# Attention scores over all 128 rows: zero-filled query tiles for each head, and the decay as two rows of k

## The chip, the cores and the metric

The kernel runs on one core of one Trainium2 chip. The metric is the device time of one execution in microseconds (us). The engines are named in the profile as PE (TensorE matmuls), PEld (TensorE weight loads), DVE (VectorE), ACT (ScalarE), POOL (GpSimd) and SP (SyncE, which issues most transfers).

## The reference, cut to what matters

A decoder trunk of two layers over 512 tokens of width 1024. The even layer has two groups of heads side by side, the odd layer has one; each layer ends in an expert-retrieval part (PEER), which the change leaves alone. Heads are 64 wide.

```python
# even layer, group A: 8 heads; an indexer picks the keys that a query may use
li = einsum('bthd,bsd->bths', q_idx, k_idx) * 64 ** -0.5          # 8 indexer heads, one shared k
iscore = einsum('bths,bth->bts', relu(li), w_idx)                 # top 128 keys of it are kept
s = q_lat . ckv * 64 ** -0.5 + bias(dist)                         # scores of group A on the kept keys
# even layer, group B: 4 heads, two softmax maps each, difference of the two
# odd layer, forgetting attention: 16 heads
cum = cumsum(log_sigmoid(f_logit), axis=1)
s = einsum('bthd,bshd->bhts', q, k) * 64 ** -0.5 + cum[t] - cum[s]
p = softmax(where(s_pos <= t_pos, s, -1e30))
```

The term `cum[t]` is the same for all keys of a query and drops out of the softmax; the kernel adds only `-cum[s]`.

## The kernel before

Tokens lie in four blocks of 128. Projections give q and k transposed: a chunk of 128 output columns holds two heads of 64, in partitions 0 to 63 and 64 to 127, with the 512 tokens along the free axis. Where precision matters a tensor is kept as a pair, its fp32r rounding and the rest (`split`, `split_to`: one ScalarE copy, lines 161 and 164, and one VectorE subtraction, lines 162 and 165), and a product is three fp32r passes (`mm3`, lines 147 to 149). Group A and group B take plain fp32 copies of q and k, where a product shows as two instructions of TensorE (line 465).

A unit is one head and one block of queries. Its scores (`scores`, line 459) contract over the 64 partitions of the head, with q as the stationary operand of 64x128 and up to 512 keys moving. There are 24 indexer units (8 heads, blocks 1 to 3), 32 units of group A, 32 matrices of group B and 64 units in the odd layer. After the scores of a group A unit one more pass adds the mask of the kept keys (line 760). After those of an odd unit one more pass adds the decay: `selR` is a constant tile of ones and zeros that picks the two rows of head h out of `cum` (its rounding in row h, its rest in row 32 + h), so line 1013 is a fourth pass over all 128 partitions. `selR` is loaded as two transfers of 512 KB ahead of the odd attention (lines 983 to 986).

Units run as a software pipeline of four or five steps (`run_units`): scores with mask and exp, the division by the sum, the transpose, the product with v. Between units a filler issues steps of the projections still to come (1.8 a unit in the odd layer), and a background list issues steps of the adaLN sums of the next sub-layers: 64 loads of 128x512 in the odd layer, two a unit, each with one VectorE instruction (lines 237 to 241). q and k of a pair of heads have two buffers each, so the projections run up to one pair ahead. The adaLN loads have three buffers of their own in the odd layer (`araw`), the projection weights have three raw buffers (`raw`, in `stream`) and three for each half of the split. The order of instructions on every engine and queue is fixed when the kernel is built, by a scheduler that follows the order of the program and its own costs; `issue_after` puts an instruction behind another one.

Lines that the prediction names: 161, 162 (splits), 465 (fp32 scores), 495 (transposes), 729 (a 128-row fp32 product with ones, in group A's stage), 800 (the copy of 64x512 out of PSUM), 1013 (the decay pass).

## Time and profile before

| What | Value |
|---|---|
| Median of three runs | 3238.81 us (3231.16 to 3241.28) |
| Profiled execution | 3246.8 us, span 3245.0 us |
| PE busy | 3159.7 us, 97% of the span |
| PEld busy | 2698.1 us, 83% |
| DVE busy | 2564.9 us, 79% |
| ACT busy | 1355.3 us, 42% |
| POOL busy | 683.2 us, 21% |
| Mean granted TensorE clock | 0.987 of full speed |

The rows come from one profiled execution, and the times in them are counted from the start of its span. A matmul's row gives its start and a modelled end; matmuls overlap in the pipeline, so the pace of TensorE is read from start to start. By the starts of the score instructions the indexer lies at 57 to 110 us, group B at 143 to 215, group A at 232 to 322 and the odd attention at 1709 to 1928.

### The profile page before, as it was taken

To read this page: it belongs to the slowest core of one execution; us is meant where nothing else is said; L and a number is where in the kernel's file an instruction comes from. 1 tells how busy PE (TensorE), PEld (TensorE's weight loads), DVE (VectorE), ACT (ScalarE), POOL (GpSimd) and SP (SyncE) were. 2 spreads that over 40 slices of the span, in tenths; PEclk is the share of its full clock that TensorE was granted. 3 is DMA by queue.
4 is the path that set the end of the run, shared out by engine and by line. 5 is a ranking of instruction groups with operands and counts; after the bars stand their busy time and mean duration, and the time that the engine had idled before them with its cause. 6 is when DMAs were issued, how large, how long until landed. Compare 5 with 4: busy or idle time off the path is not lost.

```text
span 3245.0 us, 45265 instructions
## 1 busy us (share of the span) xinstructions
PE 3159.7 (97%) x16480; PEld 2698.1 (83%) x16480; DVE 2564.9 (79%) x5076; ACT 1355.3 (42%) x2254; POOL 683.2 (21%) x516
## 2 busy tenths in 40 slices
PE   8999899999999999999999999999999999999998
PEld 4765788998999999887877778899988899899877
DVE  5887799997688877788757657999867777787877
ACT  4466423553333333333455564245533333333333
POOL 0000000002344444443200000000023444444331
PEclk9999999999999999999999989999999999999999
DMA  7314523568799899999645212246588999899885
GB/s 239 124 53 150 197 86 103 214 228 283 270 330 329 320 335 324 316 323 319 234 146 170 91 63 87 98 158 226 210 292 294 324 324 334 316 319 329 312 298 201
DMA packets 303967, 759.89 MB, mean 234 GB/s; under 512 B 24008, under 2 KB 124928, under 8 KB 297600
## 3 DMA queue, kind: packets, MB, share of 16 engines
q1 hardware_dynamic: 225536, 481.09, 43.1%
q0 software_dynamic: 73728, 268.47, 22.8%
q10 hardware_dynamic: 4480, 7.44, 0.7%
q8 instruction: 129, 2.11, 0.3%
q14 instruction: 94, 0.77, 0.1%
HBM read 700.01 MB, written 56.64 MB: 233 GB/s over the span
## 4 chain that ended last, share of the span: by engine, by line
PE 61%; DMA 17%; DVE 13%; issue 6%; ACT 2%; POOL 1%; SPq 0%; DVEq 0%; ACTq 0%; POOLq 0%
DMA gv<-in_peer_v_dram,eidx 9%; PE ups L149 7%; PE ups L147 7%; PE ups L148 7%; PE y L148 6%; PE y L149 6%; PE y L147 6%; PE pp L147 3%; PE pp L149 3%; PE pp L148 3%; DVE wl L162 3%; DMA raw<-in_peer_v_dram 2%; DMA gu<-in_peer_u_dram,eidx 1%; PE gps L1169 1%; DMA raw<-in_peer_uT_dram 1%
## 5 line engine op out<-in xcount | busy, mean ns | idle before, releaser
L161 ACT ACTIVATE wh<-raw 128x1024 fp32r<-128x1024 f32 x598 | 631.6, 1056 | 1026.0 <-PE ups L148 457.8
L162 DVE TENSOR_TENSOR wl<-raw,wh 128x1024 fp32r<-128x1024 f32 x598 | 728.8, 1219 | 140.4 <-ACT wh L161 138.6
L1406 POOL DMA_INDIRECT gu<-in_peer_u_dram,eidx x256 | 287.0, 1121 | 1964.4 <-DVE eidx L1265 1514.7
L149 PE MATMUL ups<-h2h,wl 128*128 128x384 f32 x2048 | 692.8, 338 | 6.4 <-DVE wl L162 6.4
L147 PE MATMUL ups<-h2h,wh 128*128 128x384 f32 x2048 | 693.6, 339 | 3.6 <-ACT gl L1046 2.4
L148 PE MATMUL ups<-h2l,wh 128*128 128x384 f32 x2048 | 689.7, 337 | 0.0
L147 PE MATMUL y<-wh,weh 128*128 128x512 f32 x1536 | 602.4, 392 | 12.9 <-ACT weh L161 7.2
L148 PE MATMUL y<-wl,weh 128*128 128x512 f32 x1536 | 605.5, 394 | 7.9 <-DVE wl L162 7.6
L149 PE MATMUL y<-wh,wel 128*128 128x512 f32 x1536 | 604.4, 394 | 0.0
L1406 POOL DMA_INDIRECT gv<-in_peer_v_dram,eidx x256 | 396.0, 1547 | 549.2 <-DVE gu L1413 358.5
L1421 DVE SCALAR_TENSOR_TENSOR acc<-gv,act,acc 128x1024 f32<-128x1024 f32 x256 | 328.0, 1281 | 164.6 <-DMA gv<-in_peer_v_dram,eidx 164.1
L147 PEld LDWEIGHTS ups<-h2h,wh 128*128 128x128 f32 x2048 | 385.8, 188 | 11.9 <-ACT gl L1046 3.1
L149 PEld LDWEIGHTS ups<-h2h,wl 128*128 128x128 f32 x2048 | 385.4, 188 | 9.9 <-DVE wl L162 9.8
L148 PEld LDWEIGHTS ups<-h2l,wh 128*128 128x128 f32 x2048 | 385.9, 188 | 6.5
L1413 DVE SCALAR_TENSOR_TENSOR gu<-gu,htm 128x1024 f32<-128x1024 f32 x256 | 311.9, 1219 | 51.9 <-DMA gu<-in_peer_u_dram,eidx 51.6
L147 PEld LDWEIGHTS y<-wh,weh 128*128 128x128 f32 x1536 | 290.6, 189 | 73.1 <-ACT weh L161 8.5
L148 PEld LDWEIGHTS y<-wl,weh 128*128 128x128 f32 x1536 | 290.2, 189 | 71.7 <-DVE wl L162 13.8
L161 ACT ACTIVATE weh<-wf 128x384 fp32r<-128x384 f32 x256 | 133.7, 524 | 498.3 <-PE y L148 345.2
L149 PEld LDWEIGHTS y<-wh,wel 128*128 128x128 f32 x1536 | 290.2, 189 | 61.9 <-DVE wel L162 1.3
L162 DVE TENSOR_TENSOR wel<-wf,weh 128x384 fp32r<-128x384 f32 x256 | 141.4, 553 | 83.1 <-ACT weh L161 82.6
L1300 DVE TENSOR_TENSOR wf<-gl,gt 128x384 f32<-128x384 f32 x256 | 139.9, 551 | 9.5 <-DMA gt<-gates 8.9
L1046 ACT ACTIVATE gl<-ups 128x384 f32<-128x384 f32 x256 | 121.4, 474 | 0.1
(388 smaller groups left out, 4251.5 us busy)
## 6 DMA issues: line engine op xcount, KB each, us to landing
raw<-in_peer_uT_dram SPq DMA_DIRECT2D x256, 512.0 KB
raw<-in_peer_v_dram SPq DMA_DIRECT2D x256, 512.0 KB
araw<-in_ada_w_dram SPq DMA_DIRECT2D x192, 256.0 KB
gates<-gst SPq DMA_DIRECT2D x48, 1024.0 KB
gt<-gates SPq DMA_DIRECT2D x32, 1536.0 KB
raw<-in_peer_wq_dram SPq DMA_DIRECT2D x32, 512.0 KB
raw<-in_odd_w_dram SPq DMA_DIRECT2D x25, 512.0 KB
raw<-in_even_w_dram SPq DMA_DIRECT2D x23, 512.0 KB
```

Of the source, the lines that this page charges most:

```text
L147: mm(out, a[0], b[0], start=start, stop=False)
L148: mm(out, a[0], b[1], start=False, stop=False)
L149: mm(out, a[1], b[0], start=False, stop=stop)
L161: self.lact = nc.scalar.activation(hi, src, AF.Copy)
L162: self.last = nc.vector.tensor_tensor(lo, src, hi.bitcast(F32), op=ALU.subtract)
L1046: nc.scalar.activation(gl, ps[:, :ND], AF.Gelu_apprx_tanh)
L1169: nc.tensor.matmul(ps[:, z], oh[:, t, 1], og[:, t, 0], start=True, stop=False)
L1300: nc.vector.tensor_tensor(wf.rearrange("p (c t) -> p c t", t=CT), gls[i].rearrange("p (c t) -> p c t", t=CT), self.gt[:, :, i % IG], op=AL ...
L1406: nc.gpsimd.indirect_dma_start(out=r, out_offset=None, in_=table, in_offset=bass.IndirectOffsetOnAxis(ap=eidx[:, k:k + 1], axis=0))
L1413: nc.vector.scalar_tensor_tensor(r, r, 1.0, htm, op0=ALU.mult, op1=ALU.mult, accum_out=act[:, k:k + 1])
L1421: nc.vector.scalar_tensor_tensor(acc, r, act[:, j:j + 1], acc, op0=ALU.mult, op1=ALU.add)
```

## The change

Each head gets its own query tile of 128 partitions, with the head's 64 rows in place and zeros in the other 64 (`head_tiles`). The zeros are written once by GpSimd; the split then writes only the head's half, so a split of 128 partitions becomes two of 64. Scores contract over all 128 partitions (`scores_full`), so the other head's rows of k meet zeros. This is done in the indexer (two generations of tiles), in group A (two) and in the odd layer (two); group B keeps its 64 rows.

In the odd layer k has a tile for each head too. In the half that the head doesn't use, the first two rows of the query tile are set to one, and the two rows of `cum` for the head are copied into the same rows of the k tile by a transfer from GpSimd's queue. The decay pass, `selR`, its two loads and its input go.

To make room, the adaLN loads of the odd layer take the shared `raw` buffers, `fT` takes one as well, and the latent's scratch `ckv` lies in `oT`, which is written only later.

```diff
+            qa = [self.head_tiles(qkp, f"qa{g}", 1, F32) for g in range(2)]
+            qz = []
+            def proj_i(b, w=None):
                 ps = self.bank(psum, "pp")
-                yield from self.proj_s_steps(chunk, hT, ps, w)
-                return self.split(qkp, [P, T], ps, tag, scale=scale)
+                yield from self.proj_s_steps(W[1 + b], hT, ps, w)
+                q = qz[b % 2]
+                for j in range(2):
+                    r = slice(j * HD, (j + 1) * HD)
+                    self.split_to(q[j][0][r], q[j][1][r], ps[r])
+                return q
+            def proj_aq(i):
...
+                    nc.scalar.activation(q[j][0][r], ps[r], AF.Copy, scale=HD ** -0.5)
...
+                    qz += [self.head_tiles(ix, f"qz{g}", 2) for g in range(2)]
...
-                        sc = self.scores(q, k, j * HD, tb, psum, last=tb == 0)
+                        sc = self.scores_full(q[j], k, tb, psum, last=tb == 0)
...
-        ckv = pool.tile([P, NTB, 256], F32, name="ckv")
+        ckv = self.oT[:, 0:2].rearrange("p a (b c) -> p (a b) c", c=256)
...
-                c["sc"] = self.scores(fl.get(f"i{h // 2}"), ki, (h % 2) * HD, tb, psum)
+                c["sc"] = self.scores_full(fl.get(f"i{h // 2}")[h % 2], ki, tb, psum)
...
+    def head_tiles(self, pool, name, parts, dt=F32R):
+        heads = []
+        for j in range(2):
+            tiles = [pool.tile([P, T], dt, name=self.nm(f"{name}{z}{j}"), bufs=1) for z in "hl"[:parts]]
+            for a in tiles:
+                self.nc.gpsimd.memset((a if dt == F32 else a.bitcast(F32))[(1 - j) * HD:(2 - j) * HD], 0.0)
+            heads.append(tiles)
+        return heads
+    def scores_full(self, q, k, tb, psum, last=True):
+        ps = self.bank(psum, "sc")
+        n = (tb + 1) * P
+        t = slice(tb * P, (tb + 1) * P)
+        if len(q) == 1:
+            self.nc.tensor.matmul(ps[:, :n], q[0][:, t], k[0][:, :n], start=True, stop=last)
+        else:
+            self.mm3(ps[:, :n], (q[0][:, t], q[1][:, t]), (k[0][:, :n], k[1][:, :n]), True, last)
+        return ps
...
-            selR = mp.tile([P, 16, P], F32R, name="selR")
-            qkp = s2.enter_context(self.pool("qk", bufs=2))
+            qkp = s2.enter_context(self.pool("qk"))
+            gens = [[self.head_tiles(qkp, x, 2) for x in "qk"] for g in range(2)]
+            for q, k in gens:
+                for j in range(2):
+                    nc.gpsimd.memset(q[j][0].bitcast(F32)[(1 - j) * HD:(1 - j) * HD + 2], 1.0)
...
-                fT = fp.tile([16, T], F32, name="fT")
+                fT = self.stream.tile([P, D], F32, tag="raw", name=self.nm("fT"))[:16, :T]
...
-                for z in range(2):
-                    raw = self.load(I["sel"][:, z * D:(z + 1) * D])
-                    with self.tc.issue_after(lead[0]), self.tc.issue_after(lead[1]):
-                        nc.scalar.activation(selR[:, z * 8:z * 8 + 8].rearrange("p a b -> p (a b)"), raw, AF.Copy)
...
+            def proj_qk(i):
+                q, k = gens[i % 2]
+                for x, chunk, scale in ((q, W[i], HD ** -0.5), (k, W[8 + i], None)):
+                    ps = self.bank(psum, "pp")
+                    yield from self.proj_s_steps(chunk, hT, ps)
+                    for j in range(2):
+                        r = slice(j * HD, (j + 1) * HD)
+                        self.split_to(x[j][0][r], x[j][1][r], ps[r], scale)
+                for j in range(2):
+                    h, o = 2 * i + j, (1 - j) * HD
+                    nc.gpsimd.dma_start(k[j][0].bitcast(F32)[o:o + 2], cum.bitcast(F32)[h:h + 33:32])
                 return q, k
...
-            self.bg = [self.ada(layer, m, ah, psum) for m in (2, 4, 3, 5)]
+            self.bg = [self.ada(layer, m, ah, psum, "tr", 0) for m in (2, 4, 3, 5)]
...
-                    sc = self.scores(q, k, j * HD, tb, psum, last=False)
-                    nc.tensor.matmul(sc[:, :n], selR[:, 2 * i + j], cum[:, :n], start=False, stop=True)
+                    sc = self.scores_full(q[j], k[j], tb, psum)
```

## Rows read from the trace of the kernel before

**Rows 1.** Busy time by stage; the first line names the columns.
```profile
core 0: us, PE busy (x) PEld busy (x) DVE busy (x) ACT busy (x) POOL busy (x), PEclk, DMA share, GB/s
...
57.00:110.00 53.00, 53.00 (x259) 37.91 (x258) 33.04 (x59) 23.04 (x47) 0.00 (x0) 1.00 0.38 125
110.00:143.00 33.00, 33.00 (x152) 26.61 (x150) 31.36 (x79) 11.24 (x15) 0.00 (x0) 1.00 0.45 145
143.00:215.00 72.00, 70.78 (x323) 47.22 (x324) 69.58 (x209) 46.63 (x117) 0.00 (x0) 1.00 0.15 52
...
232.00:322.00 90.00, 86.00 (x343) 50.61 (x342) 64.70 (x153) 58.77 (x149) 0.00 (x0) 0.96 0.42 139
...
1640.00:1675.00 35.00, 32.67 (x153) 26.41 (x151) 19.87 (x36) 21.42 (x39) 0.00 (x0) 1.00 0.41 135
...
1709.00:1800.00 91.00, 91.00 (x434) 67.92 (x434) 70.81 (x167) 49.82 (x121) 0.00 (x0) 0.96 0.53 176
1800.00:1860.00 60.00, 60.00 (x282) 43.52 (x280) 37.04 (x92) 34.13 (x82) 0.00 (x0) 0.95 0.22 71
1860.00:1928.00 68.00, 65.63 (x288) 47.80 (x288) 35.40 (x94) 40.70 (x99) 0.00 (x0) 0.87 0.10 32
```

**Rows 2.** Timeline of PE, an odd unit: start us, duration us, instruction.
```profile
1845.98 0.40 PE L149 MATMUL pp<-hTh,wl 128*128 128x512 f32 x1
1846.31 0.49 PE L147 MATMUL sc<-kh,qh 64*128 64x512 f32 x1
1846.64 0.39 PE L148 MATMUL sc<-kl,qh 64*128 64x512 f32 x1
1846.88 0.39 PE L149 MATMUL sc<-kh,ql 64*128 64x512 f32 x1
1847.19 0.50 PE L1013 MATMUL sc<-cum,selR 128*128 128x512 f32 x1
1847.53 0.38 PE L495 MATMUL tr<-ident,e 128*128 128x128 f32 x2
...
1848.91 0.39 PE L149 MATMUL pp<-hTh,wl 128*128 128x512 f32 x1
1849.14 0.40 PE L147 MATMUL pp<-hTh,wh 128*128 128x512 f32 x1
```

**Rows 3.** Timeline of PE, an indexer unit between projection passes.
```profile
93.46 0.28 PE L149 MATMUL pp<-wh,hTl 128*128 128x256 f32 x1
93.67 0.49 PE L147 MATMUL sc<-kih,qh 64*128 64x512 f32 x1
...
94.55 0.39 PE L147 MATMUL pp<-wh,hTh 128*128 128x256 f32 x1
94.78 0.28 PE L148 MATMUL pp<-wl,hTh 128*128 128x256 f32 x1
```

**Rows 4.** Timeline of PE, fp32 products in group A's stage.
```profile
248.49 1.12 PE L465 MATMUL sc<-kf,qf 64*128 64x512 f32 x2
249.55 1.12 PE L729 MATMUL tr<-rdg,ones 128*128 128x512 f32 x2
250.51 0.60 PE L495 MATMUL tr<-ident,e 128*128 128x128 f32 x4
```

**Rows 5.** Groups of instructions: busy us, mean ns of one, idle before.
```profile
L800 ACT ACTIVATE oT<-pp 64x512 f32<-64x512 f32 x24 | 14.2, 590 | 19.5 <-PE pp L149 10.4 <-PE pp L509 8.9
...
L162 DVE TENSOR_TENSOR kl<-pp,kh 128x512 fp32r<-128x512 f32 x8 | 5.5, 686 | 0.6 <-ACT kh L161 0.6
```

**Rows 6.** Timelines of ACT and PE at the start of a pair.
```profile
1849.47 0.59 ACT L161 ACTIVATE kh<-pp 128x512 fp32r<-128x512 f32 x1
...
1850.14 0.32 PE L147 MATMUL sc<-kh,qh 64*128 64x128 f32 x1
```

**Rows 7.** Chain that ended last: start us, us, what.
```profile
1659.53 4.08 DMA raw<-in_sel_dram
```

**Rows 8.** Waits of the SP queue, 1600 to 1930 us: total, times, longest.
```profile
SPq L237 <- DVE adacc L241: 36.0, 32, 3.4
```

**Rows 9.** Timeline of PE, fp32 scores of groups B and A.
```profile
148.54 0.92 PE L465 MATMUL sc<-kf,qf 64*128 64x384 f32 x4
...
258.95 0.91 PE L465 MATMUL sc<-kf,qf 64*128 64x384 f32 x2
```

More of the change, by code (lines that the diff above doesn't have):

```diff
@@ L584, in even @@
             fl = Filler()
-            def proj_q(chunk, tag, scale=None, w=None):
+            qa = [self.head_tiles(qkp, f"qa{g}", 1, F32) for g in range(2)]
+            qz = []
+            def proj_i(b, w=None):
                 ps = self.bank(psum, "pp")
-                yield from self.proj_s_steps(chunk, hT, ps, w)
-                return self.split(qkp, [P, T], ps, tag, scale=scale)
+                yield from self.proj_s_steps(W[1 + b], hT, ps, w)
[6 more added lines that the diff above has]
+                ps = self.bank(psum, "pp")
+                yield from self.proj_s_steps(W[13 + i], hT, ps)
+                q = qa[i % 2]
+                for j in range(2):
+                    r = slice(j * HD, (j + 1) * HD)
+                    nc.scalar.activation(q[j][0][r], ps[r], AF.Copy, scale=HD ** -0.5)
+                return q
             def plain(ps, tag, scale=1.0):
-                t = qkp.tile([P, T], F32, tag=tag, name=self.nm(tag), bufs=3 if tag == "qf" else 2)
+                t = qkp.tile([P, T], F32, tag=tag, name=self.nm(tag), bufs=2)
                 nc.scalar.activation(t, ps, AF.Copy, scale=scale)
@@ L616, in even @@
                 for b in range(4):
-                    fl.add(f"i{b}", proj_q(W[1 + b], "q", w=self.early[1] if b == 0 else None))
+                    fl.add(f"i{b}", proj_i(b, self.early[1] if b == 0 else None))
                 with self.pool("ix") as ix:
+                    self.pad(ix, 32)
+                    qz += [self.head_tiles(ix, f"qz{g}", 2) for g in range(2)]
                     fl.add("ckv", self.latent([W[21], W[22]], hT, cT, ix, ep, psum))
@@ L665, in even @@
                 fl.add("uv", proj_v())
-                fl.add("a0q", proj_f(W[13], "qf", HD ** -0.5))
-                fl.add("a1q", proj_f(W[14], "qf", HD ** -0.5))
+                fl.add("a0q", proj_aq(0))
+                fl.add("a1q", proj_aq(1))
                 def unit(h, tb, c):
@@ L741, in proj_a @@
                     else:
-                        q = yield from proj_f(W[13 + i], "qf", HD ** -0.5)
+                        q = yield from proj_aq(i)
                     ps = self.bank(psum, "pp")
@@ L838, in indexer @@
         self.proj_s(None, hT, ps, self.early[0])
-        self.pad(ip, 32)
         ki = (ip.tile([P, T], F32R, name="kih"), ip.tile([P, T], F32R, name="kil"))
@@ L982, in odd @@
                 nc.vector.tensor_tensor(cum[32:48], ps[:16], cum[0:16].bitcast(F32), op=ALU.subtract)
-                for z in range(2):
-                    raw = self.load(I["sel"][:, z * D:(z + 1) * D])
-                    with self.tc.issue_after(lead[0]), self.tc.issue_after(lead[1]):
-                        nc.scalar.activation(selR[:, z * 8:z * 8 + 8].rearrange("p a b -> p (a b)"), raw, AF.Copy)
             fl = Filler()
-            def proj_q(chunk, tag, scale=None):
-                ps = self.bank(psum, "pp")
-                yield from self.proj_s_steps(chunk, hT, ps)
-                return self.split(qkp, [P, T], ps, tag, scale=scale)
-            def proj_qk(cq, ck):
-                q = yield from proj_q(cq, "q", HD ** -0.5)
-                k = yield from proj_q(ck, "k")
+            def proj_qk(i):
+                q, k = gens[i % 2]
+                for x, chunk, scale in ((q, W[i], HD ** -0.5), (k, W[8 + i], None)):
+                    ps = self.bank(psum, "pp")
+                    yield from self.proj_s_steps(chunk, hT, ps)
+                    for j in range(2):
+                        r = slice(j * HD, (j + 1) * HD)
+                        self.split_to(x[j][0][r], x[j][1][r], ps[r], scale)
+                for j in range(2):
+                    h, o = 2 * i + j, (1 - j) * HD
+                    nc.gpsimd.dma_start(k[j][0].bitcast(F32)[o:o + 2], cum.bitcast(F32)[h:h + 33:32])
                 return q, k
@@ L1004, in odd @@
             for i in range(8):
-                fl.add(i, proj_qk(W[i], W[8 + i]))
-            self.bg = [self.ada(layer, m, ah, psum) for m in (2, 4, 3, 5)]
+                fl.add(i, proj_qk(i))
+            self.bg = [self.ada(layer, m, ah, psum, "tr", 0) for m in (2, 4, 3, 5)]
             def unit(i, j, tb, c):
@@ L1503, in layout @@
     A["ntri"] = -np.concatenate([np.triu(np.ones((P, P), np.float32)), np.ones((P, T - P), np.float32)], 1)
-    sel = np.zeros((P, 16, P), np.float32)
-    for h in range(16):
-        sel[h, h] = 1
-        sel[32 + h, h] = 1
-    A["sel"] = sel.reshape(P, 16 * P)
     A["iota"] = np.arange(NK, dtype=np.float32)[None]
```

## The prediction

> **What bounds the kernel now.** I read the busy shares of the page, then the busy time by stage, then the order of TensorE's instructions inside one unit of each attention stage. On the page TensorE is the longest engine, but a busy share counts a matmul until its modelled end, so I go by start to start.
>
> The stages that the change touches are the indexer, head group A and the forgetting attention of the odd layer; group B lies between the first two. [Rows 1] give, per stage, its length and the busy time of TensorE, its weight loads, VectorE, ScalarE and (where it worked) GpSimd. In the indexer (57 to 110 us) TensorE is busy for the whole 53.0 us, VectorE 33.0, ScalarE 23.0. From 110 to 215 VectorE is nearly full (31.4 of 33, 69.6 of 72): group B and the top-k are its stage. In A (232 to 322) TensorE has 86.0 of 90, VectorE 64.7. In the odd attention (1709 to 1928, 219 us) TensorE has 91.0 of 91, 60.0 of 60 and 65.6 of 68; VectorE has 70.8, 37.0 and 35.4. So TensorE paces the odd attention and the indexer, with VectorE close behind only in the first 91 us of the odd one, where the adaLN sums of the next sub-layers run beside it.
>
> [Rows 2] show one odd unit (one head, the last 128 queries, 512 keys). Two full 128-row passes of 512 columns start 0.23 us apart (1848.91 to 1849.14). Around the unit it is 0.33 from the last projection pass to the first 64-row pass, 0.33, 0.24 and 0.31 between the score passes and to the decay pass, and 0.34 from that to the transpose. Changing between 128 and 64 rows costs about 0.1 us, and the first pass after a change about 0.1 more. The granted clock was 0.96, 0.95 and 0.87 in the three windows [rows 1], so some stretches ran at the 1.2 GHz level instead of 2.4.
>
> **The change, part by part.**
>
> *Odd scores.* A unit takes 1847.53 - 1845.98 = 1.55 us from the last projection pass to the pass behind it. With no change of rows and three passes it would be four times 0.23 = 0.92. That saves 0.63, of which 512 columns at 2.4 GHz are 0.21 and 0.42 are the changes. Over the four block widths the mean is 320 columns, 0.13, so 0.42 + 0.13 = 0.55 a unit, and 64 units (16 heads by 4 query blocks) give 35 us of TensorE time.
>
> *Indexer.* [Rows 3]: 1.32 us from the pass before a unit to the second behind it, where five passes at the plain pitch would be 0.12 + 3 x 0.23 + 0.12 = 0.93. That is 0.39 a unit, 24 units, 9.4 us. TensorE is full here, so nearly all of it reaches the stage's end. The saving is carried through the next stages: the top-k behind it is fixed VectorE work that then starts earlier, and TensorE is full up to 143 us. I take 8.
>
> *Group A.* [Rows 4]: two 64-row fp32 instructions take 1.06 (248.49 to 249.55), two 128-row ones of the same width 0.96. With about 0.1 each on entering and on the first pass behind, by [rows 2, 3] alike, it is 0.3 a unit, 32 units, 9.6 us. But TensorE waits here (4 us idle by [rows 1]) and the chain through the softmax counts, so I take half, 5; bounds 0 and 9.6. The query's eviction becomes two ScalarE instructions, four more in all; ScalarE has 58.8 of 90.
>
> *More splits.* An instruction on 64 partitions takes as long as one on 128: 590 ns for 64x512 on ScalarE, and 686 for 128x512 on VectorE [rows 5]. In the odd layer each of 8 pairs has its q and its k split in two halves, four instructions on each engine for two: 16 more on ScalarE (9.4 us) and 16 more on VectorE (11.0 us); the indexer gets four of each (2.4 and 2.7), covered by VectorE's 20 idle us there.
>
> *What of the 35 us reaches the end.* I go window by window, spreading the 64 units and the new splits by time (a window's share of 219).
> - First 91 us, 27 units: TensorE 91 - 27 x 0.55 = 76.1. VectorE 70.8 + 4.6 = 75.4. Two engines that both need 76 and hand work to each other don't both stay full; at 90% for VectorE the stage takes 84. Saves 7 (bounds 0 and 14.9).
> - Next 60 us, 17 units: TensorE 60 - 9.4 = 50.6, VectorE 37.0 + 3.0, ScalarE 34.1 + 2.6. TensorE is still longest by 10 us. Saves 8.
> - Last 68 us, 20 units: TensorE at most 11 less. Here projections run out and the softmax chain and the lower clock (0.87) take over. Saves 4 (bounds 0 and 11).
> Together 19.
>
> *The decay rows.* 16 small transfers from GpSimd's queue, two a pair, write two rows of k. GpSimd has nothing else in either attention ([rows 1]: 0.00), so nothing is queued behind them. They write partitions that the split doesn't write; they need only the matmuls of the pair two before, a whole pair (219 / 8 = 27 us) earlier. Cost 0. If they were ordered behind the split, each pair's first score would wait for a landing. Today it starts 0.67 us after the k split begins [rows 6]. The nearest landing is 4.08 us [rows 7], so 7 pairs would cost at most some 29 us.
>
> *Memsets.* 12 on GpSimd in the even layer and 20 in the odd one, of 512 columns or so; no row shows one of that size. Nearest is the 686 ns of [rows 5]: 8 and 14 us. They lie beside work that the first score needs anyway: two projections of 24 passes, 48 x 0.23 = 11 us, before the indexer's at 57 us, and in the odd layer 96 value passes more, 33 us in all. Cost 0 to 3, I take 1, for the even layer where the cover is short.
>
> *The adaLN loads move into the shared weight buffers.* 64 loads of 256 KB shared three own buffers; now they share three with the projection weights. Today they already wait for their own buffers: 36.0 us over 32 waits on the SP queue [rows 8]. After, a weight load can't run three ahead, only about three allocations. A late weight costs ScalarE or VectorE a wait in their queue, then the softmax behind it. Eight weight loads lie in that stretch; each is covered by the two split copies ahead of it. Cost 0 to 8 x 4.08 = 33; I take 1, because the adaLN sums have the rest of the stage to finish in.
>
> *The selector load goes.* The chain names 4.08 us for it [rows 7], but TensorE is busy 32.7 of 35 us there (1640 to 1675 us, [rows 1]) with value projections that don't need it. I take 0; bound a gain of 2.3, the idle time. The latent's scratch moved into oT, fT into the stream: no instruction more, 0.
>
> **A rule that speaks against padding.** [Rows 9]: in group B four 64-row instructions of 384 columns, two heads on the two halves, take 0.92 us, as long as the two instructions of one head in group A, 0.91. The Trainium skill (TensorE: Matmul & The Clock Gate, Part 3: Packing small matmuls) says that small-K matmuls on distinct row groups run concurrently, so that pairing them, not padding them, is the gain. In the odd stage the trace shows no such overlap: the passes of a unit follow at 0.24 and more, and neighbouring units are of one head. By that rule, had all of them overlapped, padding would give back half of 192 passes of 0.13, 13 us, and the sum would be -17; by the rows it is -30.
>
> **Sum.** -8 (indexer) -5 (A) -19 (odd) +1 +1 = -30 us. The profiled execution took 3246.8 us around a span of 3245.0, so it would be 3217; the median of the three runs is 3238.81, 8 us below the profiled one, and the saving of 0.92% put on the median gives 3209.
>
> **Rivals.**
> 1. VectorE and ScalarE take over in the odd attention, above all where adaLN runs. Then the odd part saves about 5, A 2: -8 - 2 - 5 + 2 = -13, 3226. For: VectorE's 75.4 against TensorE's 76.1. Against: from 1800 us there is room. Chance 0.15.
> 2. The adaLN sums slide into the later, emptier part and nearly all TensorE time comes back: -8 - 8 - 30 + 1 = -45, 3194. For: they have no reader before the stage's end. Against: their order on VectorE's queue is fixed. Chance 0.15.
> 3. Slower: the decay rows wait behind the k split. 7 pairs by 4.08 + 0.67 us is 33, which gives +3, 3242. It decides from 4.3 us a pair. Against: other partitions. Chance 0.06.
> 4. The weight buffers starve: half of the 33 us bound and the odd gain halved, -8 - 5 - 10 + 17 = -6, 3233. Chance 0.08.
> 5. The padded passes are no faster than 64-row ones and only the fourth goes: 64 x 0.13 = 8.5 us, less some 5 for the new splits where VectorE is near its limit: -3, 3236. Against: 0.23 at 128 rows in [rows 2]. Chance 0.05.
> 6. 64-row passes that overlapped lose that: -17, 3222. Against: [rows 2]. Chance 0.03.
>
> The forecast has 0.48. About 0.3%, 10 us, is what a measurement here can tell from no change, so faster means below 3229. Faster: 0.46 of the forecast, 0.10 of rival 1, rival 2 whole (0.15), 0.02 of rival 4 and 0.02 of rival 6, 0.75. Slower: half of rivals 3 and 4 and 0.02 of rival 5, 0.09, since their bounds go past the old time. The rest, 0.16, is within 0.3%. The range runs from just below rival 2 (3190) to rival 4 (3233); outside lie rivals 3 and 5, half of 4 and the far end of 2, under 0.2.
>
> **What would show it.** No score pass with 64 rows in the odd, indexer and A stages, and start to start 0.23 us for 512 columns through a unit. The odd attention 219 us down to some 200, the indexer 53 to 45, A 90 to 85. VectorE's share above 85% in the first part of the odd attention. Wrong if a pair's first score waits for a DMA, if SP waits for the shared buffers grow while VectorE or ScalarE wait for weights, if GpSimd's memsets end after 57 us, or if the granted clock falls well below 0.9 there.

## The result, and the profile after

The changed kernel takes 3209.09 us (median of five runs, 3199.27 to 3211.82) against 3238.81 (3229.18 to 3241.28) for the kernel before: a ratio of 0.9911, 95% interval 0.9887 to 0.9935. The forecast was 3209. The profiled execution took 3209.09 us, span 3206.9; that of before lay 8 us above its median, so the two spans differ by 38 us, of which 3.8 arose in the first and 4.2 in the second PEER part, which the change doesn't touch.

The measured difference is itself uncertain by 8 us either way. In the later measurements the kernel before has medians of 3229 to 3236 us, and a kernel that differs from the changed one only in the queue of its small transfers ("Decay rows late", below) has a ratio of 0.9934, some 21 us. That the medians meet the forecast to the microsecond is luck; some 20 to 30 us is what is shown.

Busy time by stage after, to be read against [rows 1] (the columns are the same); the lines are the indexer in two parts, group B, group A, the odd setup and the odd attention in three parts:

```profile
58.00:102.00 44.00, 44.00 (x259) 38.85 (x257) 34.75 (x60) 25.13 (x51) 0.00 (x0) 1.00 0.43 141
102.00:135.00 33.00, 32.95 (x150) 26.48 (x149) 31.86 (x81) 10.87 (x15) 0.00 (x0) 1.00 0.48 157
135.00:207.00 72.00, 70.71 (x322) 46.94 (x322) 69.52 (x208) 46.59 (x117) 0.00 (x0) 1.00 0.17 52
226.00:311.00 85.00, 78.39 (x355) 53.87 (x353) 65.76 (x159) 61.31 (x153) 0.00 (x0) 0.96 0.51 161
1619.00:1696.00 77.00, 69.02 (x299) 53.66 (x298) 37.29 (x61) 29.37 (x51) 9.67 (x19) 0.96 0.28 94
1696.00:1781.00 85.00, 76.86 (x390) 62.08 (x389) 72.27 (x169) 53.31 (x125) 3.76 (x7) 0.94 0.50 160
1781.00:1841.00 60.00, 57.75 (x297) 47.22 (x297) 45.24 (x107) 40.73 (x94) 2.15 (x4) 0.95 0.42 132
1841.00:1896.00 55.00, 48.30 (x260) 38.00 (x258) 36.35 (x96) 42.47 (x103) 0.54 (x1) 1.00 0.12 39
```

By the first instruction of each stage, before and after: from the first indexer score to the first score of group B 85.5 and 76.8 us; from there to group A's first mask pass 92.4 and 91.5; from that to the first product of the output projection 91.5 and 84.2; odd setup (first product of the odd layer to the first score) 71.3 and 76.8; odd attention (first score to the first product of the output projection) 220.8 and 200.4. That sums to -8.7 - 0.9 - 7.3 + 5.5 - 20.4 = -31.8. The first indexer score comes 1.1 us later, but over all kernels below it lies between 56.5 and 57.6 us with the old even layer and between 56.8 and 59.1 with the new one, so not much of that is the change.

The passes of an odd unit after, timeline of PE, which answers to [rows 2]:

```profile
1701.78 0.48 PE L147 MATMUL sc<-kh,qh 128*128 128x512 f32 x1
1702.10 0.39 PE L148 MATMUL sc<-kl,qh 128*128 128x512 f32 x1
1702.33 0.40 PE L149 MATMUL sc<-kh,ql 128*128 128x512 f32 x1
1702.56 0.40 PE L147 MATMUL pp<-hTh,wh 128*128 128x512 f32 x1
```

From one score pass to the next, and on to the projection, it is now 0.23 us, where [rows 2] had 0.24 to 0.33; the first pitch, 0.32, is that of a pass behind a transpose. But TensorE now waits. Waits of PE in the odd attention (what waited, for whom, us in total, times, longest):

```profile
PE tr L495 <- ACT e L808: 3.3, 5, 1.3
PE pp L147 <- ACT pth L497: 2.7, 5, 1.2
PE sc L147 <- ACT e L477: 2.5, 2, 2.2
PE sc L147 <- ACT kh L161: 2.3, 4, 0.8
```

All idle time marked on PE in this stage is 16.7 us after and 3.1 before. No wait names a decay transfer. GpSimd's memsets in the even layer end at 34.4 us, before the first score, and the granted clock is 0.94 or more in the three parts, so three of the prediction's four signs of being wrong didn't show. The fourth did, in small: ScalarE waits for the loads of projection weights, which it didn't before.

```profile
ACT wh L161 <- DMA raw<-in_odd_w_dram: 4.0, 5, 1.0
```

The odd setup has a new hole: windows, a part of PE's timeline, and the waits of SP's queue for the release of a raw buffer.

```profile
1650.00:1654.00 4.00, 0.58 (x5) 0.32 (x4) 0.23 (x1) 2.99 (x5) 0.00 (x0) 1.00 0.38 129
1654.00:1660.00 6.00, 4.65 (x9) 1.30 (x10) 2.59 (x3) 3.08 (x5) 0.00 (x0) 0.50 0.00 1
...
1655.35 4.45 PE L1020 MATMUL tr<-tri,z 128*16 128x512 f32 x8 [4.09 <-DVE z L1015]
1659.72 1.45 PE L147 MATMUL pp<-wh,hTh 128*128 128x512 f32 x3
...
SPq L169 <- PE tr L1005: 11.0, 1, 11.0
SPq L169 <- PE tr L1020: 8.1, 1, 8.1
```

TensorE stands 4.09 us for z, the granted clock goes to 0.50, and the sums with tri (line 1020) run at that level. Lines 1005 and 1020 are the readers of fT and of tri, which hold two of the three raw buffers (tri held one before as well, fT is new there); two loads of value weights wait 11.0 and 8.1 us for them, so TensorE has no value projection to fill the hole with. Before, the same wait was short:

```profile
PE tr L979 <- DVE z L974: 1.0, 1, 1.0
```

### The profile page after: what moved, and what is told of

Its sections match the earlier page's. It is cut to its first block, busy times and chain, and to the rows that moved or that the text cites. A ratio compares the mean times of both kernels' runs of the same rounds, so it can differ in the third digit from the quotient of the medians.

```text
span 3206.9 us, 45322 instructions
## 1 busy us (share of the span) xinstructions
PE 3106.1 (97%) x16416; PEld 2689.4 (84%) x16416; DVE 2576.4 (80%) x5096; ACT 1367.1 (43%) x2276; POOL 705.8 (22%) x564
## 4 chain that ended last, share of the span: by engine, by line
PE 67%; DVE 14%; DMA 13%; issue 3%; ACT 2%; POOL 0%; SPq 0%; DVEq 0%; ACTq 0%; POOLq 0%
PE ups L149 9%; PE ups L147 9%; PE ups L148 9%; PE y L148 8%; PE y L149 8%; PE y L147 8%; DMA gv<-in_peer_v_dram,eidx 5%; PE pp L147 3%; PE pp L149 3%; PE pp L148 3%; DMA araw<-in_ada_w_dram 2%; DVE wl L162 2%; DMA raw<-in_peer_v_dram 2%; PE gps L1210 1%; DMA gu<-in_peer_u_dram,eidx 1%
## 5 line engine op out<-in xcount | busy, mean ns | idle before, releaser
L147 PEld LDWEIGHTS y<-wh,weh 128*128 128x128 f32 x1536 | 289.4, 188 | 71.1 <-ACT weh L161 10.7
L1341 DVE TENSOR_TENSOR wf<-gl,gt 128x384 f32<-128x384 f32 x256 | 140.2, 552 | 10.2 <-DMA gt<-gates 9.6
L1213 ACT ACTIVATE gst<-gps 128x512 f32<-128x512 f32 x192 | 104.1, 596 | 40.2 <-PE gps L1211 31.2
```

The source lines that it names most:

```text
L147: mm(out, a[0], b[0], start=start, stop=False)
L1213: nc.scalar.activation(st[:, :, lt:lt + 4], ps.rearrange("p t i -> p i t"), AF.Copy, scale=1.0 / GSC)
L1341: nc.vector.tensor_tensor(wf.rearrange("p (c t) -> p c t", t=CT), gls[i].rearrange("p (c t) -> p c t", t=CT), self.gt[:, :, i % IG], op=AL ...
```

## The experiments

One view carries most of what follows, worked out for each kernel from PE's timeline of the odd attention. From start to start of its instructions, the time splits into the columns that each streams (at 2.4 per ns: in this stage passes of 384 and of 512 columns follow one another at 0.176 and 0.227 us, 0.05 us for 128 columns), the rest of each step where that rest is under 0.45 us (changes of rows, the pitch of small passes, slow columns), and the rest where it is longer. A step is a row of the timeline, which merges equal instructions that follow each other, so "long" holds waits and some 13 to 22 us of merged transposes and small products; by single instructions it would be 5.2 us before, 7.9 without the fourth pass, 20.5 after and 11.4 with slower sums. Differences of the two long columns agree within 3 us. The low clock's loss is the sum over stretches of 2 us of 2 us times one minus the granted share, at most what the low clock cost; it lies within the other columns. The net is the stage less that loss.

```
kernel                 odd att.  columns  short  long   low clock   net
before                   220.8     139.2   65.2  16.4     15.4     205.4
even part alone          222.0     139.7   66.2  16.1     16.5     205.5
shared adaLN alone       229.2     139.5   67.6  22.1     22.2     207.0
no fourth pass           201.5     131.2   53.7  16.5      6.8     194.7
padding, fourth kept     203.6     139.9   36.1  27.7      6.8     196.8
after                    200.4     131.1   35.7  33.5      8.5     191.9
odd part alone           201.8     131.2   35.6  35.1      9.6     192.2
own buffers              195.4     130.6   36.2  28.7      8.5     186.9
thin sums                189.4     130.6   31.5  27.3      3.4     186.0
slower sums              184.5     130.6   34.1  19.8      4.9     179.6
```

The second line runs the odd layer of before again, the line of the odd part alone that of after: the split repeats within 1.6 us. The whole kernel is less steady: the first PEER part, which no run changes, took 1243 to 1259 us in these profiles. So I take small differences from the stages and give the ratios beside them.

Each line is one execution, and the low clock is where executions differ most. The profiled one of before has a mean granted clock of 0.987 over the whole program, where 68 other executions of that kernel have 0.9908 in the mean. So the net carries more than the low-clock column. The same net can be had for every execution, as its span times its mean granted clock; its medians are given below as "whole net", and are 3199 to 3202 us for the kernel before in its four measurements.

**The two layers apart.** One kernel takes the odd layer's part of the diff, the other the even layer's.

> The kernel before with the odd layer's part of the change alone (padded tiles for q and k, decay rows, no fourth pass, adaLN loads in the shared buffers, fT in a shared buffer). The two traces put the odd attention 20.5 us shorter and its setup about 1.5 us longer, so theory A (both layers gain, each by its own TensorE time) gives -16 to -20 us against the kernel before, some 3221. Theory B (the odd part trades the wait for row changes for VectorE and buffer waits, and most of the gain lies in the even layer) gives -5 to -10, some 3231.

> The kernel before with the even layer's part alone (padded query tiles in the indexer and in group A, the latent's scratch in oT). By theory A the two stages give 8 us each less 1 us of a later start: -13 to -16, some 3224, and with the odd part alone it adds up to the whole change's -30 within 4 us. If group A is set by its chain through the softmax, as the forecast's half of 9.6 us assumed, -11 to -13. Theory B: -20 or more.

Odd part: 3226.17 against 3232.78 us, ratio 0.9963 [0.9943, 0.9982]. Even part: 3215.66, 0.9947 [0.9924, 0.9970]. By stages the even part gives -8.7, -0.9 and -7.3, the odd part +4.8 in the setup (76.1 us) and -19.0 in the attention; together -31.1, as the whole change. For the even part that is theory A. The odd part's time, 7 us less by the medians and 12 by the ratio, lies in theory B's range or between the two; its stages give -14.2. By the whole net both parts give 14 us (3186.0 and 3185.9 against 3200.2), so the gain doesn't lie mostly in the even layer, as theory B had it. The odd part gives less than the first expectation had, since the setup costs more than the 1.5 us that I had read, and its mean granted clock is lower (0.9885 against 0.9904).

**Shared adaLN buffers alone.**

```diff
-            self.bg = [self.ada(layer, m, ah, psum) for m in (2, 4, 3, 5)]
+            self.bg = [self.ada(layer, m, ah, psum, "tr", 0) for m in (2, 4, 3, 5)]
```

> The kernel before with one edit: the 64 adaLN loads of the odd attention use the three shared raw buffers instead of three of their own. The forecast took +1 us with bounds of 0 and 33. By the trace of the changed kernel, where these loads end 15 us later within the stage and no projection waits long for a weight: 0 to +3, 3239 to 3242, with the adaLN sums ending later in the stage. If weights starve (the forecast's rival): +10 to +20 and TensorE waiting on weight copies. If a slower adaLN stream frees VectorE in the first part and pays: -3 to -6.

3236.54 against 3232.78 us, ratio 1.0017 [1.0001, 1.0033]. The odd attention is 8.4 us longer: 1.6 net and 6.8 of low clock. Windows of its three parts, with granted clocks of 0.92, 0.86 and 0.92:

```profile
1704.00:1789.00 85.00, 83.35 (x388) 61.94 (x388) 61.04 (x146) 44.02 (x106) 0.00 (x0) 0.92 0.47 148
1789.00:1849.00 60.00, 58.83 (x259) 44.08 (x257) 41.16 (x96) 32.89 (x78) 0.00 (x0) 0.86 0.44 143
1849.00:1933.00 84.00, 80.75 (x366) 58.40 (x365) 43.27 (x115) 51.00 (x124) 0.00 (x0) 0.92 0.10 32
```

My expectation of 0 to +3 was too low for the stage. The long gaps grow by 5.7 us, and the weights do come late, if not as often as the starving rival needs: ScalarE, which didn't wait for their loads before, now does.

```profile
ACT wh L161 <- DMA raw<-in_odd_w_dram: 6.1, 5, 1.9
```

Over all executions the whole net is unchanged (3198.3 against 3200.2) and the mean granted clock lower, 0.9883 against 0.9904, some 7 us. So here the low clock is no accident of the profiled execution.

**No fourth pass.**

```diff
-                    sc = self.scores(q, k, j * HD, tb, psum, last=False)
-                    nc.tensor.matmul(sc[:, :n], selR[:, 2 * i + j], cum[:, :n], start=False, stop=True)
+                    sc = self.scores(q, k, j * HD, tb, psum)
```

> The kernel before without the decay pass after the odd scores; the scores stay on 64 rows. It leaves the decay term out of the odd layer's scores, so its output is not the reference's. If the changes between 64 and 128 rows are the larger part of the gain (the forecast: 0.42 of 0.55 us a unit), only the pass itself goes, 0.13 us on the mean of 64 units, 8.5 us of TensorE, of which by the forecast's own ratio (19 of 35) 5 reach the end: -3 to -8, some 3234, and the stretch from the last score pass to the transpose still takes 0.3 us. If the fourth pass is what paid and padding is worth nothing: -16 to -20, some 3221.

3217.01 against 3232.78 us, ratio 0.9948 [0.9931, 0.9966], odd attention -19.3: the numbers of the theory that I had held against my own. The table says what they are made of. The columns go down by 8.0 us, as forecast, the long gaps stay within 3 us, and the short gaps lose 11.5, of which the low clock's loss of 15.4 going to 6.8 may be 8.6. Without the clock it is -10.7 (whole net -13.9), so all of the pass reaches the end, not 19 parts in 35. The drop of the low clock is one of the two executions profiled: over all of them the mean granted clock is 0.9909 without the pass and 0.9904 with it. That padding is worth nothing doesn't follow; the next run has it.

**Padding alone.** Query tiles padded as in the change, k one pair tile, the fourth pass kept, adaLN loads shared, fT in a softmax tile.

```diff
-                    sc = self.scores(q, k, j * HD, tb, psum, last=False)
+                    sc = self.scores_full(q[j], k, tb, psum, last=False)
                     nc.tensor.matmul(sc[:, :n], selR[:, 2 * i + j], cum[:, :n], start=False, stop=True)
```

> The kernel before with zero-padded query tiles in the odd layer alone: k stays one pair tile, the decay stays a fourth pass, the adaLN loads share the raw buffers (for room), and fT lies in a tile of the softmax. It is to be read against the run with shared adaLN buffers alone, whose odd attention took 229.2 us, 22.2 of them lost to the lower clock level (one minus the granted share, summed over the stage), so 207.0 without. Theory A (changes of rows are the larger part of the gain: 0.42 of 0.55 us a unit, of which some half reaches the end): 190 to 195 without the clock's loss, -5 to -10 us against the kernel before as a whole. Theory B (the fourth pass made nearly all of the gain; what padding frees on TensorE is given back in waits for VectorE and ScalarE, whose splits doubled): 201 to 205 without the clock's loss, 0 to +5 as a whole.

3217.33 against 3229.01 us, ratio 0.9970 [0.9952, 0.9989]. The odd attention takes 203.6 us, 25.6 below the kernel with shared buffers alone; its net is 196.8, between the two theories and 10.2 below. The short gaps fall by 31.5 us, 0.49 a unit, where the forecast had 0.42; up to 15.4 of them are the low clock (22.2 to 6.8), which leaves at least 0.25 to the changes of rows. The traces narrow it: of the steps into, inside and just behind a unit's score passes, those outside the low clock and without a wait exceed their columns by 0.58 us a unit with shared buffers and by 0.26 here (0.66 before, 0.22 after), so an estimate of the changes is 0.3 to 0.4 us a unit, 21 to 26 us for 64 units. The long gaps rise by 5.6. The Trainium skill (TensorEngine Tiling (Array Packing), Key Properties) says that a change of the tiling mode drains TensorE; this trace agrees that the change has a price, that one, and no run shows whether a drain makes it.

So each half alone is worth a lot, and they don't add. With the passes padded, dropping the fourth one took the stage from 203.6 to 200.4: 8.8 us of columns less, 5.8 of long gaps more. The other way round it is no more: from the kernel without the fourth pass (201.5, net 194.7) to the changed one, padding and what comes with it brought 1.1 us, 2.8 net.

**Decay rows late.**

```diff
-                    nc.gpsimd.dma_start(k[j][0].bitcast(F32)[o:o + 2], cum.bitcast(F32)[h:h + 33:32])
+                    nc.scalar.dma_start(k[j][0].bitcast(F32)[o:o + 2], cum.bitcast(F32)[h:h + 33:32])
```

> The changed kernel with the two transfers of decay rows of each pair issued from ScalarE's queue, behind the copies of that pair's k, in place of GpSimd's. It prices the forecast's rival of decay rows that come late: 4.08 + 0.67 us a pair for 7 pairs, 33 us, would bring it to 3242. If the filler has other projection passes to put in that place, half of that or less: +8 to +16 against the changed kernel, 3217 to 3225. If nothing waits for them: 3209 again.

3209.39 against 3229.01 us, ratio 0.9934 [0.9916, 0.9951], odd attention 202.1, net 193.6. It doesn't price the rival: the scheduler issued the transfers ahead of the copies here too (for the pair whose scores begin at 1785.39 us at 1764.11 and 1776.74, the copies of its k at 1783.60 and 1787.44). What late rows would cost stays open; that they aren't late in the changed kernel is shown by its waits.

**The setup's tiles.**

```diff
-                fT = self.stream.tile([P, D], F32, tag="raw", name=self.nm("fT"))[:16, :T]
+                fT = ep.tile([P, T], F32, tag="e", name=self.nm("fT"), bufs=self.e_bufs)[:16]
...
-                tri = self.stream.tile([P, D], F32, tag="raw", name=self.nm("tri"))
-                nc.sync.dma_start(tri[:, :T], I["ntri"])
+                tri = ep.tile([P, T], F32, tag="e", name=self.nm("tri"), bufs=self.e_bufs)
+                nc.sync.dma_start(tri, I["ntri"])
```

> The changed kernel with fT and tri of the odd setup in tiles of the softmax (the tag e, idle then) in place of two of the three shared raw buffers. By the trace, the setup from the first product of the odd layer to the first score took 71.3 us before and 76 to 77 after, with TensorE waiting for value weights whose loads wait for those buffers. If the buffers are the cause: 69 to 72 us again, and -4 to -6 us against the changed kernel as a whole, 3204. If the cause is GpSimd's 20 memsets or the missing loads of the selector: no change, 76.

3203.88 against 3229.01 us, ratio 0.9924 [0.9902, 0.9946]. The ratio can't tell it from the change, the stage can: 70.3 us for 76.8, with TensorE busy for 67.05 of 71 and the clock at 1.00. GpSimd's memsets (9.83 us) are still there, so it was the buffers. Of the two tiles it was fT: the kernel with padding alone keeps tri in the ring, as the kernel before did, and has fT in a softmax tile, and its setup takes 70.7 us, with this wait for z:

```profile
PE tr L1002 <- DVE z L997: 1.1, 1, 1.1
```

```profile
1621.00:1692.00 71.00, 67.05 (x302) 53.21 (x301) 37.63 (x61) 29.86 (x52) 9.83 (x19) 1.00 0.31 101
```

**Group B padded too.**

```diff
-                            sc = self.scores(q, k, j * HD, tb, psum)
+                            sc = self.scores_full(q[j], k, tb, psum)
```

> The changed kernel with group B's queries zero-padded to 128 rows as well, one tile for each of its two maps. In the rows of before, four 64-row instructions of two maps take 0.92 us at 384 columns, and two 128-row ones of that width about 0.75 (0.96 at 512), so two maps would take 1.5: some 0.6 us more for each of 16 pairs of matrices, 10 us of TensorE. If 64-row passes of two maps share the array (the rule that speaks against padding): group B's stage +4 to +10 us, for TensorE has only a few us of slack there. If they don't: 0 or a gain, -2 to -6.

3203.39 against 3229.01 us, ratio 0.9922 [0.9894, 0.9951]. Timelines of PE, the scores of two maps at 384 columns and what starts behind them, in the changed kernel and in this one:

```profile
158.62 0.92 PE L465 MATMUL sc<-kf,qf 64*128 64x384 f32 x4
159.47 0.33 PE L495 MATMUL tr<-ident,e 128*128 128x128 f32 x1
```

```profile
159.73 1.45 PE L961 MATMUL sc<-kf,qbh 128*128 128x384 f32 x4
161.01 0.27 PE L495 MATMUL tr<-ident,e 128*128 128x128 f32 x1
```

0.85 us become 1.28. The rule of the Trainium skill that the forecast weighed (TensorE: Matmul & The Clock Gate, Part 3: Packing small matmuls) holds in this place: two maps on the two halves overlap, and padding takes that away. Group B's stage grew by 0.5 us only (91.5 to 92.0). The likely reason is that VectorE sets it (69.52 of 72 us above); the expected +4 to +10 took TensorE's 1.3 idle us for all its slack.

**Own adaLN buffers.** On top of the setup's tiles, room is made for three buffers: the two heads share one kl tile, the ones move to ql, and `cum` goes through DRAM (the last isn't in the cut below).

```diff
-            gens = [[self.head_tiles(qkp, x, 2) for x in "qk"] for g in range(2)]
+            gens = [[self.head_tiles(qkp, x, p) for x, p in (("q", 2), ("k", 1))] for g in range(2)]
             for q, k in gens:
+                kl = qkp.tile([P, T], F32R, name=self.nm("klo"), bufs=1)
                 for j in range(2):
-                    nc.gpsimd.memset(q[j][0].bitcast(F32)[(1 - j) * HD:(1 - j) * HD + 2], 1.0)
+                    nc.gpsimd.memset(q[j][1].bitcast(F32)[(1 - j) * HD:(1 - j) * HD + 2], 1.0)
+                    k[j].append(kl)
...
-            self.bg = [self.ada(layer, m, ah, psum, "tr", 0) for m in (2, 4, 3, 5)]
+            self.bg = [self.ada(layer, m, ah, psum, "tr", 3) for m in (2, 4, 3, 5)]
```

> The changed kernel with room made for three own adaLN buffers in the odd attention and none of the setup's tiles in the raw ring: the ones go into ql in place of qh, so that both heads share one kl tile; cum is written once to DRAM and its rows are copied from there; fT, tri and cum lie in softmax tiles. By the runs so far: setup 70 to 71 us for 76.8 (shown by the run with the setup's tiles), odd attention less the sharing's 1.6 us and some of its low-clock time, 185 to 191 us net of the clock's loss against 191.9. Sum -6 to -12 against the changed kernel, 3198 to 3203. If sharing costs nothing beside the padded passes: setup alone, -6, attention 192 net again.

3194.96 against 3230.18 us, ratio 0.9885 [0.9867, 0.9902]. Setup 71.2, odd attention 195.4 and net 186.9, against 202.7 and 192.4 in the kernel before this edit (with the setup's tiles). So sharing cost some 5 to 7 us beside padded passes as well, if the edits that made the room cost nothing themselves, which wasn't measured apart. ScalarE's waits for the weights' loads are gone.

**The sums on GpSimd.**

```diff
-                    nc.vector.scalar_tensor_tensor(acc, raw, self.cact[:, kt:kt + 1], acc, op0=ALU.mult, op1=ALU.add)
+                    nc.gpsimd.tensor_scalar(raw, raw, self.cact[:, kt:kt + 1], None, op0=ALU.mult)
+                    nc.gpsimd.tensor_tensor(acc, acc, raw, op=ALU.add)
```

> The kernel with own buffers, with the odd attention's adaLN sums on GpSimd (a multiplication and an addition for each load) in place of VectorE's one instruction. In the changed kernel these take VectorE 746 ns each, 49 of them in the stage, some 40 us with the first ones. If VectorE's load is what keeps the stage at 192 us net where TensorE has about 181 us of work without waits (191.9 less the 13.6 us by which its marked idle grew): 180 to 188 us net. If GpSimd's work slows VectorE's own, or the decay rows come late behind the sums on GpSimd's queue: 192 to 200 us net. If VectorE was not the limit: 191 again.

3285.55 against 3230.18 us, ratio 1.0179 [1.0155, 1.0202], odd attention 272.0 us. PE's longest wait, and GpSimd's groups of instructions (busy us, mean ns):

```profile
PE tr L249 <- POOL adacc L243: 72.8, 7, 12.8
...
L242 POOL TENSOR_SCALAR araw<-araw,cact 128x512 f32<-128x512 f32 x47 | 75.0, 1596 | 0.6 <-DMA araw<-in_ada_w_dram 0.5
L243 POOL TENSOR_TENSOR adacc<-adacc,araw 128x512 f32<-128x512 f32 x49 | 62.8, 1281 | 3.7
```

A load costs GpSimd 2.88 us where VectorE took 0.746. The small product that reads a finished sum stands at a fixed place in TensorE's order, placed for the faster sums, and there TensorE waits up to 12.8 us, seven times. It says nothing on what VectorE's load costs.

**The sums thinned.** Seven of eight sum instructions copy one column only.

```diff
-                    nc.vector.scalar_tensor_tensor(acc, raw, self.cact[:, kt:kt + 1], acc, op0=ALU.mult, op1=ALU.add)
+                    nc.vector.tensor_copy(acc[:, :1], raw[:, :1])
```

> The changed kernel with the adaLN sums of the odd attention thinned: of each group of eight loads only the first is multiplied in full, for the other seven VectorE copies one column, so the sums of four modulations are left out and the output is not the reference's; loads, buffers and TensorE's part stay. It takes some 33 us of VectorE out of the stage without GpSimd. If VectorE's load sets what is left after padding: odd attention 180 to 186 us net of the clock's loss against 191.9, with TensorE's marked idle down from 16.7 to below 8 us. If the chain through the softmax or ScalarE sets it: 189 to 192 and idle 14 to 17.

3198.24 against 3230.18 us, ratio 0.9906 [0.9888, 0.9924]; odd attention 189.4, net 186.0, marked idle 15.1. The net is at the far end of the first theory, the idle with the second. So some 6 us net of the stage hang on VectorE's load while the buffers are shared (the 5 of low clock are this execution's, and the whole net, 3168.0, is only 0 to 5 below the changed kernel's 3168.4 and 3173.0); what its load costs without the shared buffers this run doesn't show.

**Slower sums.** The kernel with own buffers and one number changed.

```diff
-OB = 2
+OB = 1.2
```

> The kernel with own buffers, with the adaLN sums of the odd attention issued 1.2 a unit in place of 2, so that they end after some 53 of the 64 units in place of 32. With own buffers VectorE had 71.4 of the first 85 us and 32.0 of the last 50, and thinning these sums to an eighth gave 6 us net of the clock's loss and 5 of low-clock time. If VectorE's load in the first part is the limit there and the last part has room: first half shorter, odd attention 183 to 185 us net against 186.9, -2 to -5 us as a whole, 3190 to 3193. If the chain through ScalarE and the transposes sets the pace in every part: 187 net, and the same time within 2 us; if the later sums get in the way of the thinner last part: 188 to 192.

3181.23 against 3235.66 us, ratio 0.9834 [0.9809, 0.9859], clear of the change's interval and of that of own buffers (whole net 3153.3, 49 us below before). The odd attention takes 184.5 us, net 179.6, and the long gaps are 19.8 us for 28.7. More than I had expected. Windows of its first two parts, behind those of the kernel with own buffers:

```profile
1698.00:1783.00 85.00, 78.85 (x401) 65.10 (x401) 71.37 (x171) 52.95 (x128) 3.03 (x6) 0.92 0.54 169
1783.00:1843.00 60.00, 57.76 (x306) 47.64 (x305) 48.00 (x111) 41.18 (x97) 2.53 (x5) 0.97 0.30 94
...
1689.00:1774.00 85.00, 83.54 (x453) 67.90 (x452) 72.56 (x176) 62.07 (x150) 3.54 (x7) 1.00 0.43 138
1774.00:1834.00 60.00, 59.37 (x328) 48.94 (x327) 54.17 (x127) 41.89 (x99) 2.52 (x5) 1.00 0.47 154
```

In the first 85 us VectorE is no less busy than with two sums a unit (72.56 and 71.37), but 25 of its instructions are sums (line 241) where 37 were, and TensorE and ScalarE get more done (83.54 and 62.07 us for 78.85 and 52.95). In the next 60 VectorE has 54.17 us where it had 48.00, and TensorE loses nothing by it. One number was changed, so it is the rate of the sums and of their loads that made the difference; which of the two, this run doesn't part.

## Why the prediction was right, and where it was right by luck

The total and its sign came out: -30 forecast, -29.7 measured, 3209 and 3209. The mechanism, TensorE time in the three stages, was right too. That the numbers meet so closely is luck: the interval reaches from -21 to -37, the forecast has no term for the clock, and the setup took 5.5 us for which nothing had been set, which group A and the attention made up in the profiled executions. Term by term:

- **Indexer -8:** measured -8.7, and -0.9 in group B's stage behind it. Right.
- **Group A -5:** -7.3. The mechanism was right, the size a little off: I halved 9.6 us because TensorE had 4 idle us there. Some 1.7 of the difference is less low clock in the even stages (5.1 us lost before, 3.4 after), so it is -5.6 without.
- **Odd TensorE time, 35 us (0.55 a unit):** right, and shown by two runs apart: 8.0 us of columns without the fourth pass (8.3 forecast), and short gaps that fall by 31.5 us without the row changes, 16 to 31.5 of them not the clock's, 21 to 26 by the estimate at full clock (27 forecast).
- **What of it reaches the end, 19:** 20.4 in the profiled executions, but 6.9 of it is the clock, for which no term stood, and the profiled execution of before had more low clock than most; net it is 13.5. The columns and short gaps fell by 8.1 + 29.5 us and the long gaps rose by 17.1. By the first scores of the pairs, the first four took 108.2 us for 114.9 and the last four 92.2 for 105.9, net of the clock 6.7 and 6.9 less. What is missing against 19 is about the price of the shared buffers: with own buffers the net is 18.5 below before.
- **Shared adaLN buffers +1:** mis-sized. Alone they cost 8.4 us of the odd attention (1.6 net), and some 5 to 7 beside padded passes. It lay inside the bounds (0 to 33); "covered by the two split copies ahead of it" was the step that failed, by ScalarE's waits for the loads.
- **fT into the stream, "no instruction more, 0":** the step that was wrong. It adds no instruction, but it takes a buffer from the ring through which the value weights come. The setup grew by 5.5 us, 3.4 of them low clock, and came back whole when fT and tri left the ring; with fT alone outside it, in the kernel with padding alone, it was never longer. The selector's load, with its 4.08 us on the chain [rows 7], is gone in that kernel as well, for a gain of 1.0 us at most, as bounded.
- **More splits, memsets, decay rows:** 64x512 takes 687 ns on VectorE, as long as 128x512 [rows 5]; memsets take 0.52 us each (0.69 taken) and aren't seen in the first score; no wait for decay rows.

Of the rivals, the first (VectorE and ScalarE take over) is half of what happened: TensorE's marked idle grew by 13.6 us and the long gaps by 17.1, most of it in waits for ScalarE. The second (nearly all comes back) was not reached by the change. With own buffers and the adaLN sums spread it is nearly so: 220.8 to 184.5 us is -36, but 10.5 of it is the clock, and net it is -25.8 of the 35. The step from own buffers to spread sums, 7.3 net by one number, shows that the pace of these sums and their loads held back a good part of the saving; the chain through ScalarE alone would have left it at 187. The decay rows' rival fell by the trace, its price is untested. The fifth (the fourth pass is all) fell by padding alone, whose net is 10.2 below the kernel with shared buffers; but with the shared buffers and the doubled splits to pay for, the odd attention of the change is only 2.8 net below that without the fourth pass. The sixth (lost overlap) fell in the odd layer by padding alone too; the overlap is real in group B.

What stays open: how ScalarE's and VectorE's doubled splits share in the long gaps that are left, and whether two heads' 64-row passes, woven like group B's maps, would do as well as padding in the odd layer. Neither was tried. Open too is what sets TensorE's clock in this stage.

## What to carry to other kernels

When a change frees time on the engine that sets the pace, the next limit may be background work that is issued at a fixed rate: look at its rate before giving up the rest (one number was worth 11 us in the stage here). A tile that moves into a shared ring costs nothing in instructions and can still cost a stage its weights: name what else comes through that ring while the tile is held. And of two edits that free the same engine, measure each alone: net of the clock, -10.7 us from the kernel before and -10.2 from the one with shared buffers became -13.5 and -15.1 together. Last, compare the mean granted clock of all executions before a profile's low clock is counted as a gain.

## What was not expected of the hardware

One execution's clock misled. In the profiled one of before, the granted clock stood at the 1.2 GHz level in three stretches of the odd attention, from 1737.6, 1795.6 and 1904.8 us, and cost up to 15.4 us; in the profiled ones with the fourth pass gone, or with the row changes gone, it cost 6.8, and in the changed kernel 8.5. That looks like a gain by the clock. Over all executions it isn't one: the whole program's mean granted clock is 0.9908 before (68 executions, 0.987 in the profiled one), 0.9909 without the fourth pass, 0.9912 with padding alone and 0.9888 in the five of the changed kernel. The change as a whole lost some 0.002 of 3200 us, about 6, by the clock, and saves 26 to 32 in whole net (3168.4, and 3173.0 with the decay rows on ScalarE's queue, against 3199 to 3202). The kernels with shared adaLN buffers alone (0.9883) and with the odd part alone (0.9885) are low as well, those with own buffers (0.9902) and slower sums (0.9920) are not; but padding alone shares the buffers too. So what lowers the clock in this stage was not settled; in the setup it fell while TensorE stood for 4.09 us.

On GpSimd, a multiplication of 128x512 by a column took 1596 ns and an addition 1281, against 746 for both in one VectorE instruction; at that price idle GpSimd was no place for the sums.
